# A hybrid encoder layer: TensorE's order in attention and recurrence is written by the program from a model of the other engines

## The chip, the cores and the metric

The kernel runs on one core of a Trainium2 chip. The metric is device time in microseconds (us) of one execution, the median of several; lower is better. The core has five engines that the profile names PE (TensorE: matrix products), DVE (VectorE), ACT (ScalarE), POOL (GpSimd) and SP (SyncE, which here only issues DMA transfers). Each works off its own queue in order and waits for the others by semaphores. SBUF is the on-chip memory of 128 partitions; a product lands in PSUM, of which one bank holds 128 x 512 float32 and must be copied out ("evicted") by another engine before it is used again.

## The reference, cut to what matters

One layer on 1024 frames of width 1024, all in float32.

```python
u = rms_norm(h, mix_norm_gain)
aq, ak, av, dqkv, dgate, da, db = split(u @ w_in)        # 8 attention heads of 64, 4 delta heads of 128
# A: every chunk of 64 frames looks at itself and the 8 chunks before it
q, k   = rms_norm(aq), rms_norm(ak)                      # per head
scores = q k^T * 64**-0.5 + rel_bias, masked to the band
o_att  = rms_norm(softmax(scores) @ v)
# B: gated delta rule, chunks of 64 in the reference; any chunk length gives the same result
dq, dk, dv = silu(causal_conv(dqkv));  q, k = l2_norm(dq) * 128**-0.5, l2_norm(dk)
T = I + strict(tril(beta k k^T * decay))                 # per chunk and head
value, k_cumdecay = T^-1 (beta v), T^-1 (beta k exp(decay))
for each chunk:                                          # S is the state, 128 x 128 per head
    v_new = value - k_cumdecay @ S
    o     = q_decay @ S + tril(q k^T * decay) @ v_new
    S     = S * chunk_decay + k_tail^T @ v_new
o_dn = rms_norm(o) * silu(dgate)
h = h + concat(o_att, o_dn) @ w_out
h = h + relu(rms_norm(h) @ w_ff1)**2 @ w_ff2
```

## The kernel before, in words

Frames are cut into 8 tiles or chunks of 128. The kernel goes through stages in the order of TensorE's time: the projection of dk (from 6 us), a small one for decay and beta, dq, dv, the gate, ak, aq, and six of the eight tiles of av; then attention and recurrence together (349 to 587 us), the output product `op` beside their end (562 to 662), and the two products of the feed-forward part (663 to 1281). Every large product is made of three (high x high, high x low, low x high part: `mm3`).

*Attention* goes over 16 tiles (g, t): g is a group of four heads, t one of 8 tiles of 128 frames. For each pair of heads pp (0 or 1), `score` makes the products with the keys, `t_sb` for the newest two tiles of keys and `t_sa` for up to three older ones, VectorE adds the bias and takes the row's extreme, and ScalarE the exponential (pages `t_pb`, `t_pa`). `value` transposes these on TensorE (`t_tpb`, `t_tpa`, into the two banks of `ps_t`), has them copied to SBUF (`t_tb` and the first `t_ta` by ScalarE, the second `t_ta` by VectorE), and multiplies by the values into one bank, `t_o`. The products into `t_o` use half of the array's columns each (128 x 64), so that two heads go side by side. `finish` turns `t_o` once more (`t_on`), and `turn` turns the normed result (`t_tpo`) for the output product.

*The recurrence* goes over 8 chunks c. Ahead of attention, beside the projections, `delta_prep` makes the matrices T and inverts their 32 x 32 diagonal blocks on VectorE (they go through memory: `x_dr`, `y_dr`, `a_dr`). In the stage, `delta_merge(c)` puts the blocks of one chunk together: first 32 x 32 products (`m_p`, four at a time on two corners of 32 x 32 of the array), then 64 x 64 ones (`m_tp`, `m_p`). `delta_state(c)` makes the products `c_tpv`, `c_pk`, `c_pv`, `c_pq` and `c_pS` with the state, `delta_out(c)` `c_tpq`, `c_mt`, `c_po`, and `delta_fin(c)` `c_tpo`. Each is a group of four products, one per head, in one of the two banks of `ps_d`.

What sets the order: these are Python generators, and `interleave` takes the next step from the one whose sum of given costs, divided by its weight, is least; the recurrence's own steps go in the order of a string of letters. This is the order in which the program names the instructions; a scheduler of the compiler then orders each engine's queue from it by its own model, and moves an instruction ahead of a neighbour where that model finds it ready earlier. So small groups of one kind come to stand between products of another:

```python
ORDER = "OSMOSMFSOMOSMSL"
...
    interleave((attention(after[NV - 1]), 1.0), (delta_all(ab, kT), 2.0), (values, WV))
    R, begun = out_proj()
```

At the start of the kernel, TensorE multiplies a page of ones `WARM` = 8 times (`warm`, line 111) while the first weights and the first part of x are loaded; `uh` and `wdk_h` are the high parts of x and of the first weights, made by ScalarE. ScalarE's first activation, line 185, brings a load of its function table with it.

Of the kernel before, what the change touches and what calls it, by code (L numbers as in the profile page):

```python
# [14 lines left out]
P = 128  # L15
# [7 lines left out]
ATT_D = 64  # L23
# [12 lines left out]
ORDER = "OSMOSMFSOMOSMSL"  # L36
LATE = 2
SPREAD = 5
WARM = 8
LAST = {"b22": "t1", "t3": "t2", "t4": "b22"}  # L40
RS = "a"
NV = 6
WV = 2.5
# [3 lines left out]
def hymba_kernel(  # L47
# [60 lines left out]
    nc.gpsimd.memset(ones, 1.0)  # L108
    warm = bank(ps_o, "warm")
# [51 lines left out]
    def mm3(ps, terms):  # L161
        n = 3 * len(terms)
        i = 0
        for (ah, al), (bh, bl) in terms:
            for a, b in ((ah, bh), (ah, bl), (al, bh)):
                nc.tensor.matmul(ps, a, b, start=(i == 0), stop=(i == n - 1))  # L166
                i += 1
# [8 lines left out]
    def load_xt(hf, k):  # L176
# [9 lines left out]
        nc.vector.scalar_tensor_tensor(lo, raw, mgain[:, k:k + 1], hi.bitcast(F32), ALU.mult, ALU.subtract)  # L186
        acc = squares[hf][k % 2]
# [7 lines left out]
    for k in range(NKT):  # L195
        if k:
            w_dk.append(load_w(w_in[k * P:(k + 1) * P, DK:DK + 512], f"wdk_{k}"))
        load_xt(0, k)
        if not k:
            w_dk.append(load_w(w_in[0:P, DK:DK + 512], "wdk_0"))  # L200
# [30 lines left out]
    nc.gpsimd.memset(state[0], 0.0)  # L231
# [259 lines left out]
    def delta_prep(kT, ab):  # L491
# [4 lines left out]
        for c in range(NT):  # L496
# [5 lines left out]
            kt = page("pp", n + "_kt")  # L502
            nc.vector.tensor_tensor(b4(kt), b4(tp), bc_row(ab["edec"][:, 1, h4]), ALU.mult)
            nc.sync.dma_start(out=kt_dr[c], in_=kt)
# [45 lines left out]
    def delta_merge(c, res):  # L550

        n = f"m{c}"
        Ap, Yp, s1 = (page("pp", n + k) for k in ("_ab", "_yb", "_s1"))
        A, Y = b4(Ap), b4(Yp)
        X = s1[:, 384:512].rearrange("p (h e) -> p h e", h=4)
        Yc = s1[:, 256:384].rearrange("p (h e) -> p h e", h=4)
        nc.sync.dma_start(out=Ap, in_=a_dr[c])
        for dst, src in ((X, x_dr), (Yc, y_dr)):
            nc.sync.dma_start(out=dst, in_=src[4 * c:4 * c + 4].rearrange("b r h e -> (b r) h e"))
        nc.gpsimd.memset(Yp, 0.0)  # L560
        for b in range(4):
            bs = slice(32 * b, 32 * b + 32)
            nc.gpsimd.tensor_copy(Y[bs, :, bs], Yc[bs])
        yield 0
        p1 = bank(ps_d, n + "_p1")
        for c0 in (0, 64):
            for h in range(4):
                nc.tensor.matmul(p1[c0:c0 + 32, 32 * h:32 * h + 32], A[c0:c0 + 64, h, c0:c0 + 32],
                                 Y[c0:c0 + 64, h, c0 + 32:c0 + 64], start=True, stop=True)
            nc.scalar.copy(s1[c0:c0 + 32, 0:128], p1[c0:c0 + 32, 0:128])  # L570
        yield 500
        p2 = bank(ps_d, n + "_p2")
        for c0 in (0, 64):
            cs = slice(c0, c0 + 32)
            for h in range(4):
                hs = slice(32 * h, 32 * h + 32)
                nc.tensor.matmul(p2[cs, hs], X[cs, h, :], s1[cs, hs], start=True, stop=True)
            nc.scalar.mul(Y[cs, :, c0 + 32:c0 + 64], p2[cs, 0:128].rearrange("p (h e) -> p h e", h=4), -1.0)
        yield 500
        tp = bank(ps_d, n + "_tp")  # L580
        for h in range(4):
            nc.tensor.transpose(tp[0:64, h * 64:h * 64 + 64], Y[0:64, h, 0:64], ident[0:64, 0:64])
        for h in range(4):
            nc.tensor.matmul(tp[0:64, 256 + h * 64:320 + h * 64], A[64:128, h, 0:64], Y[64:128, h, 64:128],
                             start=True, stop=True)
        x1 = s1
        nc.scalar.copy(x1[0:64, :], tp[0:64, :])
        yield 700
        p4 = bank(ps_d, n + "_p4")
        for h in range(4):  # L590
            hs = slice(h * 64, h * 64 + 64)
            nc.tensor.matmul(p4[0:64, hs], x1[0:64, hs], x1[0:64, 256 + h * 64:320 + h * 64],
                             start=True, stop=True)
        nc.scalar.mul(Y[0:64, :, 64:128], p4[0:64, 0:256].rearrange("p (h e) -> p h e", h=4), -1.0)
        res[c] = Yp
        yield 400

    def delta_state(c, ab, kTs, Ys, D):

# [8 lines left out]
        ktail = page("cv", n + "_kt")  # L608
        nc.sync.dma_start(out=ktail, in_=kt_dr[c])
# [3 lines left out]
        nc.vector.tensor_tensor(b4(rr), b4(tp), bc_row(ab["br"][:, h4]), ALU.mult)  # L613
        yield 500
        pk = bank(ps_d, n + "_pk")
        four(pk, lambda h, hs: kT[:, hs], lambda h, hs: S[:, h, :])
        for h in range(4):
            hs = slice(h * P, (h + 1) * P)
            nc.vector.scalar_tensor_tensor(
                rr[:, hs], pk[:, hs], ab["nbr"][:, 4 * c + h:4 * c + h + 1], rr[:, hs],  # L620
                ALU.mult, ALU.add)
        yield 900
# [4 lines left out]
        nc.scalar.copy(vn, pvn)  # L627
        yield 900
        pq = bank(ps_d, n + "_pq")
        four(pq, lambda h, hs: dq[:, hs], lambda h, hs: S[:, h, :])  # L630
        o = page("cv", n + "_o")
        nc.vector.tensor_tensor(b4(o), b4(pq), bc_row(ab["edec"][:, 0, h4]), ALU.mult)
        yield 900
        pS = bank(ps_d, n + "_pS")
        four(pS, lambda h, hs: ktail[:, hs], lambda h, hs: vn[:, hs])
        for h in range(4):
            nc.vector.scalar_tensor_tensor(
                S2[:, h, :], S[:, h, :], ab["edec"][:, 2, 4 * c + h:4 * c + h + 1],
                pS[:, h * P:(h + 1) * P], ALU.mult, ALU.add)
        D[c] = dq, dg, vn, o  # L640
        yield 900

    def delta_out(c, ab, kTs, D):
# [4 lines left out]
        dq, dg, vn, o = D.pop(c)  # L648
        Lt = decay(T, n + "_Lt", ab, h4, tri_u, tri_sr, nc.gpsimd)
        nc.gpsimd.tensor_tensor(b4(Lt), b4(Lt), bc_mask(tri_u), ALU.mult)  # L650
        yield 450
        tp = bank(ps_d, n + "_tpq")
        four_t(tp, head(dq))
        nq = rsqrt("c", sumsq(tp, "c", tp, n + "q"), 4, 1.0, EPS, n + "q")
# [4 lines left out]
        yield 500  # L659
# [3 lines left out]
        nc.vector.tensor_tensor(att, mp, Lt, ALU.mult)  # L663
        yield 900
        po = bank(ps_d, n + "_po")
        four(po, lambda h, hs: att[:, hs], lambda h, hs: vn[:, hs])
        nc.vector.tensor_tensor(o, o, po, ALU.add)
        ss = sumsq(po, "c", o, n)
# [5 lines left out]
        yield 900  # L674

    def delta_fin(c, D):
        n = f"c{c}"
        o, dg = D.pop(c)
        tp = bank(ps_d, n + "_tpo")
        four_t(tp, head(o))  # L680
        if c % TPH == 0:
            mix[c // TPH][1] = quarter(f"mixd{c // TPH}")
        nc.vector.scalar_tensor_tensor(q4(mix[c // TPH][1])[:, :, (c % TPH) * P:(c % TPH + 1) * P], b4(tp), dng,
                                       b4(dg), ALU.mult, ALU.mult)
        yield 500

    def delta_all(ab, kTs):

        Ys, D = {}, {}
        merge = delta_merge(0, Ys)  # L690
        yield from merge
        merge = delta_merge(1, Ys)
        for c in range(NT + LATE):
            gens = dict(S=delta_state(c, ab, kTs, Ys, D) if c < NT else iter(()),
                        O=delta_out(c - 1, ab, kTs, D) if 0 < c <= NT else iter(()),
                        F=delta_fin(c - LATE, D) if c >= LATE else iter(()), M=merge)
            merge = delta_merge(c + 2, Ys) if c + 2 < NT else iter(())
            gens["L"] = merge
            for k in ORDER:
                cost = next(gens[k], None)  # L700
# [707 lines left out]
```

## Time and profile before

| | |
|---|---|
| time, median of 3 runs | 1286.75 us (1284.92 to 1287.67) |
| the profiled execution | 1288.31 us, its span 1286.6 us |
| mean granted clock of TensorE | 0.998 of full speed |
| busy share of the span | PE 98%, DVE 73%, ACT 43%, POOL 23% |
| DMA | 160.65 MB in 129288 packets, 125 GB/s over the span |

The profile's page gives the busy time of each engine, the span in slices, the chain of work that ended last, and groups of instructions by line. A row of the timeline gives the start in us from the span's start, the time that a run of equal instructions took, engine, line, operation, tiles (written <- read), the part of the array in use (rows*columns), the shape, the number of records, and in brackets the idle time ahead of it with what ended that. A float32 product on TensorE often shows as two records.

### The profile page before, as it was taken

The page shows a single profiled execution, that of the slowest core. Times are in us where ns is not written, and L with a number is a line of the kernel's source. Part 1 is how long each engine was busy: PE and PEld are TensorE (multiplying, and loading weights), DVE is VectorE, ACT ScalarE, POOL GpSimd, SP SyncE. Part 2 cuts the span into 40 slices and gives each one's busy share as a digit, 9 for nine tenths or more (in the row PEclk, how much of TensorE's full clock was granted, in tenths as well). Part 3 has the DMA queues.
Part 4 walks back from the last instruction along what each step waited for, and adds up shares of the span by engine and source line. Part 5 has one row for each costly group of instructions (what it writes and reads, how often), then busy time and mean ns, then how long its engine had stood idle before and what let it go on. Part 6 is the DMA issues. An engine that isn't in the chain of part 4 may idle for free.

```text
span 1286.6 us, 18043 instructions
## 1 busy us (share of the span) xinstructions
PE 1260.6 (98%) x6702; PEld 1040.6 (81%) x6702; DVE 935.0 (73%) x1401; ACT 553.9 (43%) x919; POOL 293.0 (23%) x499
## 2 busy tenths in 40 slices
PE   9999999999999999989999999999999999999998
PEld 7778878788888887868877788888887888888886
DVE  7899987665046666863529876776668997897988
ACT  7233132133166664665335445444455443333331
POOL 4435461454024355523310000000000000000034
PEclk9999999999999999999999999999999999999999
DMA  6214353656492742125351433232358733422002
GB/s 223 61 44 140 100 164 112 145 147 160 144 270 79 218 109 75 42 65 163 122 166 31 151 116 129 98 110 97 105 196 318 238 93 104 131 86 95 17 33 98
DMA packets 129288, 160.65 MB, mean 125 GB/s; under 512 B 22832, under 2 KB 71984, under 8 KB 128688
## 3 DMA queue, kind: packets, MB, share of 16 engines
q1 hardware_dynamic: 111104, 137.20, 34.7%
q10 hardware_dynamic: 18096, 22.29, 5.0%
q8 instruction: 53, 0.87, 0.3%
q14 instruction: 35, 0.29, 0.1%
HBM read 111.75 MB, written 47.71 MB: 124 GB/s over the span
## 4 chain that ended last, share of the span: by engine, by line
PE 72%; DVE 8%; issue 2%; DMA 2%; POOL 1%; ACT 1%; POOLq 1%; SPq 0%; ACTq 0%; DVEq 0%
PE q L1087 22%; PE p L1183 20%; PE op L166 5%; PE av_ps L166 3%; PE aq_ps L166 3%; PE g_ps L166 3%; PE t_o L865 3%; PE ak_ps L166 2%; PE t_sb L793 1%; PE t_sa L793 1%; PE t_tpb L844 1%; PE t_tpa L855 1%; PE c_mt L461 1%; PE c_pS L461 1%; DVE ml L148 1%
## 5 line engine op out<-in xcount | busy, mean ns | idle before, releaser
L1255 POOL TENSOR_TENSOR y<-y,y 128x1024 f32<-128x1024 f32 x6 | 19.3, 3243 | 591.7 <-DVE y L1251 572.9
L1251 DVE TENSOR_TENSOR y<-y,p 128x1024 f32<-128x1024 f32 x46 | 55.2, 1218 | 5.4 <-PE p L1183 4.5
L808 DVE CUSTOM_DVE_ANT_0 t_pb<-t_sb,biasn 128x256 f32<-128x256 f32 (+1 forms) x64 | 25.4, 402 | 43.6 <-POOL biasn L720 25.4
L166 PE MATMUL op<-mh,wo_h 128*128 128x512 f32 x128 | 50.3, 393 | 0.8 <-DVE t_nm L808 0.3
L166 PE MATMUL op<-ml,wo_h 128*128 128x512 f32 x128 | 50.1, 391 | 0.0
L166 PE MATMUL op<-mh,wo_l 128*128 128x512 f32 x128 | 48.3, 391 | 0.0
L823 ACT ACTIVATE t_pb<-t_pb,t_nm 128x256 f32<-128x256 f32 (+1 forms) x64 | 31.6, 494 | 22.7 <-DVE t_nm L817 12.7
L966 DVE TENSOR_TENSOR h<-op,op_x 128x512 f32<-128x512 f32 x16 | 10.8, 688 | 30.7 <-PE op L166 30.7
L793 PE MATMUL t_sb<-ks,t_q 128*128 128x256 f32 (+1 forms) x144 | 30.4, 308 | 0.8 <-DMA t_q<-q_dr 0.5
L973 POOL TENSOR_TENSOR op_q<-op_q 128x512 f32<-128x512 f32 x14 | 20.1, 1439 | 48.0 <-ACT op_q L972 47.8
L166 PEld LDWEIGHTS op<-mh,wo_h 128*128 128x128 f32 x128 | 24.0, 188 | 7.4 <-issue 1.0
L817 DVE CUSTOM_DVE_ANT_0 t_pa<-t_sa,biaso,t_nm 128x384 f32<-128x384 f32 (+2 forms) x48 | 26.3, 547 | 4.4 <-PE t_sa L793 2.9
L865 PE MATMUL t_o<-t_ta,vt 128*64 128x128 f32 x240 | 27.3, 293 | 1.4 <-DVE t_ta L858 1.1
L166 PEld LDWEIGHTS op<-mh,wo_l 128*128 128x128 f32 x128 | 24.0, 188 | 5.2 <-issue 0.2
L166 PEld LDWEIGHTS op<-ml,wo_h 128*128 128x128 f32 x128 | 24.0, 188 | 4.9
L166 PE MATMUL g_ps<-uh,wg_h 128*128 128x512 f32 x64 | 25.2, 394 | 1.4 <-ACT wg_h L147 1.4
L826 ACT ACTIVATE t_pa<-t_pa,t_nm 128x384 f32<-128x384 f32 (+2 forms) x48 | 26.4, 550 | 0.1
L793 PE MATMUL t_sa<-ks,t_q 128*128 128x256 f32 (+2 forms) x128 | 25.5, 310 | 0.3 <-DVE t_nm L808 0.3
L166 PE MATMUL g_ps<-uh,wg_l 128*128 128x512 f32 x64 | 25.2, 394 | 0.4 <-POOL wg_l L148 0.4
L166 PE MATMUL dq_ps<-uh,wdq_h 128*128 128x512 f32 x64 | 25.5, 398 | 0.0
L166 PE MATMUL dv_ps<-uh,wdv_l 128*128 128x512 f32 x64 | 25.4, 397 | 0.0
L166 PE MATMUL aq_ps<-waq_h,uh 128*128 128x512 f32 x64 | 25.3, 401 | 0.0
(1102 smaller groups left out, 4353.8 us busy)
## 6 DMA issues: line engine op xcount, KB each, us to landing
wa<-in_w_ff_dram SPq DMA_DIRECT2D x32, 512.0 KB
a<-in_w_ff_dram SPq DMA_DIRECT2D x32, 512.0 KB
b<-f_dr SPq DMA_DIRECT2D x32, 512.0 KB
f_dr<-yy ACTq DMA_DIRECT2D x16, 512.0 KB
t_q<-q_dr SPq DMA_DIRECT2D x30, 256.0 KB
f_dr<-zz ACTq DMA_DIRECT2D x13, 512.0 KB
ks<-k_dr SPq DMA_DIRECT2D x16, 256.0 KB
wo_r<-in_w_out_dram SPq DMA_DIRECT2D x16, 256.0 KB
```

Of the source, the lines that this page charges most:

```text
L166: nc.tensor.matmul(ps, a, b, start=(i == 0), stop=(i == n - 1))
L461: nc.tensor.matmul(ps[:, hs], lhs(h, hs), rhs(h, hs), start=True, stop=True)
L793: nc.tensor.matmul(o, q[m][:, i * P:(i + 1) * P], k[:, c], start=(m == 0), stop=(m == 1))
L808: nc.vector.tensor_tensor_reduce(sb[:, c], bk[:, c], new[g][pp][:, c], -1.0, 3.0e38, ALU.add, ALU.min, nm[:, 4 + i:5 + i])
L817: nc.vector.tensor_tensor_reduce(sa[e][:, 0:wa], bk[:, 0:wa], old[g][i][:, 384 - wa:384], -1.0, nm[:, 4 + i:5 + i], ALU.add, ALU.min, nm[: ...
L823: nc.scalar.activation(sb[:, c], sb[:, c], AF.Exp, bias=m, scale=-1.0, accum_out=T["sums"][:, 4 + i:5 + i])
L826: nc.scalar.activation(sa[e][:, 0:wa], sa[e][:, 0:wa], AF.Exp, bias=m, scale=-1.0, accum_out=T["sums"][:, i:i + 1])
L865: nc.tensor.matmul(po[64 * e:64 * e + 64, pp * P:(pp + 1) * P], vt[k0 + j][:, 64 * h:64 * h + 64], (ta[e] if j < na else tb)[:, c:c + P], ...
L973: nc.gpsimd.tensor_tensor(acc, acc, sq, ALU.add)
L1087: nc.tensor.matmul(part(ps, q), l[:, s], r, start=(k + m == 0), stop=(k == 3 and m == 2))
L1183: nc.tensor.matmul(part(ps[q], 0) if by_rows else part(ps[q // 2], q % 2), l[:, s], part(r, k), start=(i + k + m == 0), stop=(i + k + m == 4))
L1251: nc.vector.tensor_tensor(y[i][m], y[i][m], ps[m], op)
```

## The change

*The order.* A class `Clock` holds a model: the time on TensorE (`pe`), the intervals in which VectorE, ScalarE and POOL are taken (`on`), and the time from which each PSUM bank is free again (`give`). `attention` no longer yields to `interleave`. It has a loop of its own that keeps a list of what may come next: steps of the recurrence, `multiply` (the products into `t_o` for both pairs of heads of a tile), `later` (`finish` and `turn`), `flip` (the transposes), `score`, the rest of `av`, and, once the values are all turned, steps of the output product, which is now a generator. It takes the one that the model says can start first, by rank where several can. The loop runs under `manual_schedule` for TensorE, so the order of the program is TensorE's order; the other engines' queues are still ordered by the scheduler.

*The evictions* are named under `high_priority`, and the copies of `t_tb` and `t_ta` go to the one of VectorE and ScalarE that the model says is done sooner (`sooner`).

*The merges.* `delta_low` does the 32 x 32 steps for four chunks at once (`l_p`, 32 products behind each other); for the first four chunks it stands ahead of the stage, beside the projections. `delta_merge` keeps the 64 x 64 steps. The blocks are loaded from memory in more and smaller transfers.

*Less work.* In chunk 0, where the state is zero, `c_pk` and `c_pq` go, and the state is copied, not added to. In chunk 7 `c_pS` and its operand `kt` go.

*The start.* `WARM` is 11; an activation of one column of ones (`turn_on`) stands ahead of all others on ScalarE; the load of the first weights `wdk_0` is named earlier. In the norm ahead of the feed-forward part, a reciprocal gets priority.

The diff, cut to its core:

```diff
-ORDER = "OSMOSMFSOMOSMSL"
-WARM = 8
+WARM = 11
+DELTA = 71e3
+LATENCY, MARGIN = 250, 400
-WV = 2.5
+class Clock:
+    def pe(self, cost):
+        self.now += cost
+        return self.now + LATENCY
...
+    def sooner(self, costs, *after):
+        def end(e):
+            t = max((self.now,) + after)
+            for a, b in self.free[e]:
+                if a <= t < b:
+                    t = b
+            return t + costs[e]
+        return min(costs, key=end)
+
+    def give(self, pool, t):
+        self.banks[pool].pop(0)
+        self.banks[pool].append(t)
+        return t + MARGIN
...
+    turn_on = cpool.tile([P, 1], F32, name="turn_on")
+    nc.scalar.activation(turn_on, ones[:, 0:1], AF.Square)
...
+    def delta_low(b, W, tag):
...
+        for c in range(4):
+            q = 16 * b + 4 * c
+            for k in range(4):
+                nc.sync.dma_start(out=Y[c // 2][32 * k:32 * k + 32, c % 2, :, 32 * (k % 2):32 * (k % 2) + 32],
+                                  in_=y_dr[q + k])
+            for r0 in (0, 64):
+                nc.sync.dma_start(out=XA[r0:r0 + 32, c], in_=x_dr[q + r0 // 32])
+                nc.sync.dma_start(out=XA[r0 + 32:r0 + 64, c], in_=a4[c, r0 + 32:r0 + 64, :, r0:r0 + 32])
...
+            held(places, lambda c, h, hs: nc.tensor.matmul(
+                p1[rs, hs], XA[rs2, c, h, :], Y[c // 2][rs2, c % 2, h, 32:64], start=True, stop=True))
+            with tc.high_priority():
+                nc.scalar.copy(s1[rs], p1[rs])
...
-        pk = bank(ps_d, n + "_pk")
-        four(pk, lambda h, hs: kT[:, hs], lambda h, hs: S[:, h, :])
+        if c:
+            yield max(t, when["state"]), "d"
+            pk = bank(ps_d, n + "_pk")
+            four(pk, lambda h, hs: kT[:, hs], lambda h, hs: S[:, h, :])
...
-            nc.scalar.copy(*w3)
+            t = pe(nb * 218)
+            e = clock.sooner(dict(s=140 + nb * 220, v=160 + nb * 270), t)
+            with tc.high_priority():
+                copy[e](*w3)
+            t = give("t", on(e, 140 + nb * 220, t, ahead=True))
...
+        while True:
...
+            best = min(todo, key=lambda p: (max(p[0] - clock.now, 0), p[1]))
+            if best[0] > clock.now:
+                clock.now = best[0]
...
+            elif k == "multiply":
+                for n in units[multiplied:multiplied + 2]:
+                    multiply(*n)
+                    pe(218 * size[multiplied])
...
-                with tc.issue_after(m.ins):
+                with tc.issue_after(m.ins), tc.high_priority():
                     nc.vector.reciprocal(r_col, r_col)
...
-        (delta_prep(kT, ab), 0.35))
-    interleave((attention(after[NV - 1]), 1.0), (delta_all(ab, kT), 2.0), (values, WV))
-    R, begun = out_proj()
+        (chained(delta_prep(kT, ab), (1000 for _ in delta_low(0, W, "pp"))), 0.35))
+    clock.reset()
+    with tc.manual_schedule(engines={mybir.EngineType.PE}):
+        rest = attention(after[NV - 1], delta_all(ab, kT, W), values, lambda: out_proj(result))
+    for _ in rest or ():
+        pass
```

How this moves TensorE's instructions shows best at one tile's products into `t_o`. This is TensorE's queue at the tile (g, t) = (0, 5) in the order before; the names are the transposed pages `t_ta` and `t_tb` of two heads and the value tiles `vt`:

```order
L461 MATMUL c_po<-c_vn,c_att 128x128 x4
L865 MATMUL t_o<-t_ta_5134,vt_3469 64x128
L844 MATMUL t_tpb_5343<-ident,t_pb_5076 128x128 x4
L865 MATMUL t_o<-t_ta_5140,vt_3469 64x128
L865 MATMUL t_o<-t_ta_5134,vt_3799 64x128
L865 MATMUL t_o<-t_ta_5140,vt_3799 64x128
L865 MATMUL t_o<-t_ta_5134,vt_3802 64x128
L865 MATMUL t_o<-t_ta_5140,vt_3802 64x128
L865 MATMUL t_o<-t_tb_5128,vt_3813 64x128 x2
L865 MATMUL t_o<-t_tb_5128,vt_3816 64x128
L461 MATMUL c_pq<-state_297,c_jq 128x128 x4
L865 MATMUL t_o<-t_tb_5128,vt_3816 64x128
```

And the same tile now:

```order
L672 MATMUL m_tp<-ident,l_w_4324 64x64 x4
L674 MATMUL m_tp<-l_w_4324,m_sa 64x64 x4
L1009 MATMUL t_o<-t_ta_4674,vt_3582 64x128
L1009 MATMUL t_o<-t_ta_4680,vt_3582 64x128
L1009 MATMUL t_o<-t_ta_4674,vt_3755 64x128
L1009 MATMUL t_o<-t_ta_4680,vt_3755 64x128
L1009 MATMUL t_o<-t_ta_4674,vt_3758 64x128
L1009 MATMUL t_o<-t_ta_4680,vt_3758 64x128
L1009 MATMUL t_o<-t_tb_4616,vt_3769 64x128 x2
L1009 MATMUL t_o<-t_tb_4616,vt_3772 64x128 x2
L1009 MATMUL t_o<-t_ta_4719,vt_3582 64x128
L1009 MATMUL t_o<-t_ta_4747,vt_3582 64x128
```

The transposes `t_tpb` and the group `c_pq`, which stood inside the products of one pair of heads, are gone from there, and the second pair's products follow at once.

The merges, on TensorE again, where the second 32 x 32 products of chunk 5 stood before, at the beginning of the second group of heads:

```order
L865 MATMUL t_o<-t_tb_5737,vt_3466 64x128 x2
L461 MATMUL c_pk<-state_297,kT_654 128x128 x4
L865 MATMUL t_o<-t_tb_5762,vt_3466 64x128 x2
L577 MATMUL m_p_4622<-m_s_4547 32x32 x4
L887 MATMUL t_on<-ident,t_pb_5724 128x128 x2
L844 MATMUL t_tpb_5797<-ident,t_pb_5750 128x128 x4
L577 MATMUL m_p_4622<-m_s_4547 32x32 x4
L465 MATMUL c_tpo<-ident,c_o 128x128 x4
```

And where the second batch of them, for chunks 4 to 7, has its second product now:

```order
L515 MATMUL c_pv<-c_jv,m_yb 128x128 x4
L515 MATMUL c_pq<-state_302,c_jq 128x128 x4
L1031 MATMUL t_on<-ident,t_pb_4155 128x128 x2
L970 MATMUL t_tpb_4611<-ident,t_pb_4233 128x128 x4
L648 MATMUL l_p_4618<-l_s_4327,l_xa 32x32 x32
L515 MATMUL c_pS<-c_vn,c_kt 128x128 x4
```

Fours of 32 x 32 products between others on the whole array have become one run of 32.

The beginning of ScalarE's queue, before:

```order
L1403 UNCONDITIONAL_BRANCH
L180 DMA xt_174<-in_x_t_dram 128x512
L185 ACT_TABLE_LOAD
L185 ACTIVATE uh_0_150<-xt_174,mgain 128x512
L190 ACTIVATE xs_179<-xt_174 128x512
```

And now:

```order
L1649 UNCONDITIONAL_BRANCH
L235 DMA xt_179<-in_x_t_dram 128x512
L163 ACT_TABLE_LOAD
L163 ACTIVATE turn_on<-ones 128x1
L240 ACTIVATE uh_0_155<-xt_179,mgain 128x512
```

The table load no longer stands with the first activation that needs x, but with one that needs only the ones.

More of the change, by code (lines that the diff above doesn't have):

```diff
@@ L165, in mm3 @@
             for a, b in ((ah, bh), (ah, bl), (al, bh)):
-                nc.tensor.matmul(ps, a, b, start=(i == 0), stop=(i == n - 1))
+                nc.tensor.matmul(ps, a, b, start=(first and i == 0), stop=(last and i == n - 1))
                 i += 1
@@ L607, in delta_state @@
             nc.sync.dma_start(out=b4(t), in_=src[c])
[L608 to L609 removed]
+        if c + 1 < NT:
+            ktail = page("cv", n + "_kt")
+            nc.sync.dma_start(out=ktail, in_=kt_dr[c])
+        yield clock.now + 2000, "d"
         tp = bank(ps_d, n + "_tpv")
@@ L910, in attention, with live_add @@
-        for i in range(len(units) + lag + late):
-            if i < len(units):
-                g, t, pp = units[i]
+        size = [min(t + 1, 5) for g, t, pp in units]
+        total, spent, deltas, begun, multiplied = sum(size), 0, 0, 0, 0
+        ready, later, live = [], [], {}
+        banks = clock.banks
+        groups = delta
+        fed = next(groups)
+        def live_add(name, gen):
+            first = next(gen, None)
+            if first is not None:
+                live[name] = gen, first
```

425 lines of the change are left out of this document (296 added, 129 removed).

## The prediction

> **What bounds the kernel now.** I read the page's busy shares first, then the busy time in stretches of the attention and recurrence stage, then TensorE's instructions there in order of time.
>
> ```profile
> PE 1260.6 (98%) x6702; PEld 1040.6 (81%) x6702; DVE 935.0 (73%) x1401; ACT 553.9 (43%) x919; POOL 293.0 (23%) x499
> PE 72%; DVE 8%; issue 2%; DMA 2%; POOL 1%; ACT 1%; POOLq 1%; SPq 0%; ACTq 0%; DVEq 0%
> ...
> 349.00:400.00 51.00, 51.00 (x440) 42.78 (x441) 22.78 (x92) 28.71 (x91) 14.89 (x46) 1.00 0.75 220
> 400.00:450.00 50.00, 50.00 (x501) 43.77 (x497) 31.48 (x100) 32.12 (x93) 20.12 (x58) 1.00 0.50 154
> 450.00:500.00 50.00, 47.60 (x449) 39.93 (x448) 32.61 (x103) 29.45 (x92) 25.98 (x71) 1.00 0.39 104
> 500.00:562.00 62.00, 58.69 (x532) 50.64 (x530) 48.70 (x134) 40.00 (x109) 28.20 (x77) 0.97 0.13 36
> 562.00:590.00 28.00, 25.04 (x149) 19.63 (x148) 14.67 (x26) 11.64 (x26) 9.82 (x17) 1.00 0.44 132
> ```
>
> TensorE is busy for 98% of the span and is 72% of the chain. In the stage's stretches (columns: stretch, length, then busy PE, PEld, DVE, ACT, POOL, the granted clock, DMA) it is idle for only 0 + 0 + 2.40 + 3.31 + 2.96 = 8.7 us; VectorE is busy at most 48.70 of 62 us. So an order that only removed idle time could win 8.7 us. But a busy TensorE is not one at its peak, so I looked at how far apart the starts lie:
>
> ```profile
> 420.90 1.16 PE L461 MATMUL c_po<-c_vn,c_att 128*128 128x128 f32 x8
> 421.99 0.43 PE L865 MATMUL t_o<-t_ta,vt 128*64 128x128 f32 x2
> 422.35 0.66 PE L844 MATMUL t_tpb<-ident,t_pb 128*128 128x128 f32 x4
> 422.94 0.76 PE L865 MATMUL t_o<-t_ta,vt 128*64 128x128 f32 x9
> ...
> 423.96 1.16 PE L461 MATMUL c_pq<-state,c_jq 128*128 128x128 f32 x8
> 425.05 0.43 PE L865 MATMUL t_o<-t_tb,vt 128*64 128x128 f32 x2
> ...
> 433.61 0.38 PE L887 MATMUL t_on<-ident,t_pb 128*128 128x128 f32 x2
> 433.83 0.60 PE L844 MATMUL t_tpb<-ident,t_pb 128*128 128x128 f32 x4
> 434.26 0.49 PE L465 MATMUL c_tpq<-ident,c_jq 128*128 128x128 f32 x3
> ```
>
> The first column is the start, 128*64 the part of the array in use. Four transposes between others on the whole array take 434.26 - 433.83 = 0.43 us. The same four between two t_o groups take 422.94 - 422.35 = 0.59 us, though no idle time is shown. They pay 0.16 us for coming from and going to another array form. I did this for every matmul of the stage: the start-to-start distance, less what its kind has inside a run of one form.
>
> ```profile
> 349.28 0.33 PE L793 MATMUL t_sb<-ks,t_q 128*128 128x128 f32 x2
> ...
> 425.75 0.49 PE L855 MATMUL t_tpa<-ident,t_pa 128*128 128x128 f32 x3
> 426.00 0.49 PE L793 MATMUL t_sb<-ks,t_q 128*128 128x256 f32 x2
> ...
> 587.05 0.60 PE L465 MATMUL t_tpo<-ident,t_on 128*128 128x128 f32 x4
> ```
>
> From the first t_sb (349.28) to the last t_tpo (587.05) the form changes 174 times, and the excess there adds to 25.6 us, 0.147 us each. That is three times the idle time, and no wait shows it.
>
> **The change, part by part.**
>
> *Fewer changes of form.* I counted runs of one form in the order: 175 before and 61 now in this stretch, so 114 changes fewer. t_o now comes in 16 blocks (it had 51 runs), and the 25 runs of 32x32 products are two. At 0.147 us that is 16.8 us, all on TensorE's own path, with nothing to hide it. Bounds: 0.10 us each (what t_o loses on leaving) makes 11; 0.20 (c_pq takes 425.05 - 423.96 = 1.09 us; its records stand 0.111 us apart inside the run, and eight times that is 0.89) makes 23. I keep the mean. [...] Ahead of the stage five runs less give 5 x 0.147 = 0.7 us.
>
> *Work removed.* Chunk 0 has no state, so its c_pk and c_pq go, and so does chunk 7's c_pS: three groups of four products. A group is eight records in the trace, 0.111 us apart as above: 0.9 us, and 2.7 us for three. VectorE loses twelve 128-column operations and three 512-column ones and gains two copies, POOL issues 16 operations less, ScalarE 20; all three have idle time in every stretch above, so I cost these at nothing.
>
> *Idle time and evictions.* Evictions go ahead in their queues, and TensorE keeps the order written down even where something is not ready.
>
> ```profile
> 550.96 0.66 PE L844 MATMUL t_tpb<-ident,t_pb 128*128 128x128 f32 x4 [0.87 <-DVE mixa L904]
> ...
> 553.20 0.80 PE L855 MATMUL t_tpa<-ident,t_pa 128*128 128x128 f32 x3 [0.79 <-ACT t_tb L847]
> ...
> 565.56 0.66 PE L844 MATMUL t_tpb<-ident,t_pb 128*128 128x128 f32 x4 [0.90 <-ACT t_on L893]
> ...
> 569.53 0.76 PE L865 MATMUL t_o<-t_ta,vt 128*64 128x128 f32 x9 [1.15 <-DVE t_ta L858]
> 549.90:553.40 3.50, 1.84 (x15) 1.45 (x14) 1.78 (x6) 2.65 (x8) 1.50 (x6) 0.99 0.00 0
> 553.40:556.80 3.40, 3.40 (x21) 2.41 (x21) 2.88 (x8) 1.78 (x5) 0.00 (x0) 0.50 0.00 0
> 563.60:567.00 3.40, 2.16 (x16) 1.58 (x15) 1.37 (x4) 2.27 (x8) 1.12 (x4) 1.00 0.84 286
> ```
>
> The largest waits lie at the end, when the recurrence is over and attention alone waits for its copies. In the new order chunk 7's products stand among the last tiles, and steps of the output product follow. Idle time can fall by all 8.7 us, or grow as much where an order that can't bend meets a late copy. I take a third off: -3. After 1.66 us idle between 549.9 and 553.4 the clock fell to 0.50 for 3.4 us, which cost 1.7 us; with that cluster spread out I take -1.7 (bounds: 0, or one more such fall, +1.7).
>
> *The merges' loads.* The lower 32x32 merges of four chunks become one step; the first moves ahead of attention. SP issues 46 DMAs more in all (480 to 526 in the order). Around the start of the q projection 24 small loads stand where 7 larger ones stood, ahead of its last weights:
>
> ```profile
> 251.82 1.10 SPq L559 DMA_DIRECT2D m_s<-y_dr  x2
> 253.49 6.95 SPq L447 DMA_DIRECT2D k_dr<-ak_l  x4
> 262.77 3.09 SPq L154 DMA_DIRECT2D waq_r<-in_w_in_dram  x3
> ```
>
> At up to 0.5 us each, 17 more take 8.5 us of SP. SP has some 2.3 us free there now (the k_dr stores end at 253.49 + 6.95 = 260.44, the weights begin at 262.77), and part of the 6.95, in which two pairs of stores of the row are issued with a wait between them. If all of it showed, TensorE would wait 8.5 us for the weights, or as long for the loads themselves, since the products stand in a fixed place; hidden, it is 0. I take +1, as the queue has most of that room.
>
> *The start.*
>
> ```profile
> 1.05 3.78 PE L111 MATMUL warm<-ones 128*128 128x128 f32 x16 [1.05 <-POOL ones L108]
> 6.30 0.79 PE L307 MATMUL dk_ps<-uh,wdk_h 128*128 128x512 f32 x1 [1.47 <-ACT wdk_h L147]
> 6.89 0.63 PE L307 MATMUL dk_ps<-ul,wdk_h 128*128 128x512 f32 x1
> 7.32 0.63 PE L307 MATMUL dk_ps<-uh,wdk_h 128*128 128x512 f32 x1
> ...
> 9.88 1.46 PE L307 MATMUL dk_ps<-uh,wdk_l 128*128 128x512 f32 x4
> 11.17 1.07 PE L307 MATMUL dk_ps<-uh,wdk_h 128*128 128x512 f32 x4
> ...
> 3.20 1.28 ACT L185 ACT_TABLE_LOAD   x1 [3.20 <-DMA mgain<-in_mix_norm_gain_dram]
> ```
>
> The table load (1.28 us) moves into ScalarE's wait for x, so uh and wdk_h come 1.28 us earlier, at about 5.0. Each warm product is two records; the first is 0.37 us ahead of the second and the rest stand 0.2135 us apart (from start to start in the trace). The last of 22 would be followed at 1.05 + 0.37 + 21 x 0.2135 = 5.9, so the first real one starts 0.4 us earlier, with no gap before it. Its distance is 0.43 us at half clock; in the row at 9.88 they fall to 0.23, from 10.6 on: this is the end of the first 3.41 us stretch without a gap (553.4 lies 159 such stretches later). Without the gap that end is one stretch earlier, at 7.2. The twelve products then take until 9.3 instead of 11.2: -1.8 (bounds: -0.4 if the clock rises no sooner, -2.3). [...]
>
> *No cost or gain.* The reciprocal's priority in norm_col: the order leaves it behind the same four operations, so the row
>
> ```profile
> PE hrow L1051 <- DVE r_col L1045: 1.7, 1, 1.7
> ```
>
> stays. From ff1 on the order is nearly the same (a few VectorE operations swap), so the part behind its first product,
>
> ```profile
> 662.95 0.47 PE L1087 MATMUL q<-b11h,q_0a_h 128*128 128x512 f32 x1 [0.88 <-DVE h L966]
> ```
>
> stays within 1 us.
>
> **Sum:** -1.8 - 0.7 + 1 - 16.8 - 2.7 - 3 - 1.7 = -25.7 us, or 2.0%. The profiled execution took 1288.31 us, 1.7 more than its span of 1286.6; it would take 1262.6. The median of three runs is 1286.75, 1.56 under the profiled one; on it the sum gives 1261.
>
> **Rivals.**
>
> *New waits eat much of it.* Each of the 16 t_o blocks now needs up to six copies done at once, and one PSUM bank serves them. One wait of 1 us at each, as at 569.53, costs 16 us and makes 1277; a wait of 0.6 makes 1271. For it: that wait, and VectorE's 79% in 500 to 562. Against: two transpose groups and the scores stand between copy and use. 0.17.
>
> *The price is no price of form.* If the excess came from loading weights after a jump, it would come back elsewhere: 1261 + 16.8 = 1278. Against: the t_tpa that t_sb follows on the whole array, at 425.75, take 426.00 - 425.75 = 0.25 us for three, no excess. 0.07.
>
> *The waits all go,* 8.7 instead of 3, and the SP loads hide: 1254 or less. 0.09.
>
> *Slower:* one mechanism, the fixed order at the t_o blocks. Sixteen waits of 1.6 us cancel the gain; from 1.8 us on the kernel is slower, 1.9 us makes 1291. The longest wait of the stage now is 1.15 us. 0.04.
>
> *No change to speak of,* between those two: 0.03.
>
> *The clock falls in transposes.* The new order has a run of 23 transposes, about 2.5 us. [...] Were such runs to halve it, each fall would cost 1.7 us; three make 1266. Between 563.6 and 567.0 TensorE did little but some fifteen transposes and 1.24 us of idling, and the clock stayed 1.00; the trace speaks against it. 0.02, inside the likeliest case's range.
>
> **The numbers.** The sum as it stands, give or take 7 us for waits and loads (1254 to 1268 or so), has 0.60. Reaching to half of the first two rivals and most of the third gives 1251 to 1277 for 8 in 10. About 0.2%, 2.6 us, is what a measurement can tell from no change: faster 0.60 + 0.17 + 0.07 + 0.09 = 0.93, same 0.03, slower 0.04.
>
> **What would show it.** Right: the first dk product near 5.9 and distances of 0.23 from about 7.2; t_o in 16 blocks; four transposes 0.43 apart nearly everywhere; the first ff1 product near 637 instead of 663, and 624 us from there to the end as before. Wrong: waits at t_o or t_tpa of a microsecond each, a gap at the first aq product or the first l_p, or stretches at clock 0.50 in the stage.

## The result, and the profile after

The changed kernel is slower: 1319.55 us median of five runs (1308.9 to 1323.4) against 1286.75 (1284.92 to 1287.94), a ratio of 1.0239 (95% interval 1.0214 to 1.0265). The forecast was 1261. The profiled execution is the quickest of the five, 1308.9 us with a span of 1307.1. Its page and the stretches of the stage, in the columns shown for the kernel before:

```profile
PE 1249.8 (96%) x6684; PEld 1038.5 (79%) x6684; DVE 933.2 (71%) x1389; ACT 548.1 (42%) x899; POOL 289.9 (22%) x486
PE 57%; DVE 8%; ACT 2%; issue 2%; POOL 2%; DMA 1%; POOLq 1%; SPq 0%; DVEq 0%; ACTq 0%
...
349.00:400.00 51.00, 43.95 (x331) 36.90 (x330) 21.04 (x87) 26.55 (x87) 12.77 (x41) 0.97 0.71 209
400.00:450.00 50.00, 43.70 (x482) 39.15 (x480) 26.19 (x80) 25.54 (x72) 16.63 (x47) 0.96 0.44 126
450.00:500.00 50.00, 42.40 (x400) 37.21 (x400) 31.47 (x99) 26.43 (x81) 21.43 (x54) 1.00 0.30 81
500.00:550.00 50.00, 39.19 (x341) 35.98 (x341) 31.22 (x97) 24.76 (x77) 16.18 (x48) 0.93 0.23 64
550.00:610.00 60.00, 50.94 (x388) 43.02 (x389) 37.00 (x79) 29.36 (x70) 30.98 (x68) 0.97 0.20 62
```

TensorE is idle for 7.0 + 6.3 + 7.6 + 10.8 + 9.1 = 40.8 us of these stretches; from 349 to 610 us of the kernel before it is 9.0. No other engine is busier than before. The clock is below 1.00 in four stretches of five. The summed waits of TensorE in the stage (total, times, longest) name the place, and the last row is what the first one was before:

```profile
PE t_sb L914 <- DVE t_nm L930: 23.2, 31, 1.5
PE t_tpa L986 <- ACT t_ta L991: 3.5, 1, 3.5
PE t_tpa L986 <- ACT t_tb L976: 2.4, 4, 1.0
...
PE t_sb L793 <- DVE t_nm L808: 0.2, 1, 0.2
```

And one of the 31, in the timeline:

```profile
402.19 0.48 PE L914 MATMUL t_sb<-ks,t_q 128*128 128x256 f32 x2
...
402.71 0.42 DVE L930 CUSTOM_DVE_ANT_0 t_pb<-t_sb,biasn 128x256 f32<-128x256 f32 x1
403.06 0.08 DVE L930 DVE_READ_ACCUMULATOR2_ANT t_nm<- 128x1 f32 x1
...
403.19 0.50 PE L914 MATMUL t_sb<-ks,t_q 128*128 128x256 f32 x2 [0.53 <-DVE t_nm L930]
403.54 0.86 PE L914 MATMUL t_sa<-ks,t_q 128*128 128x384 f32 x4
```

`score` puts the newest keys' products of two heads into the two halves of one bank. The program names them as product, VectorE's reduction, product, reduction, and the second product waits until VectorE has read the first half. In the trace of the changed kernel nothing stands between the two heads' products in any of the 32 banks. Before, the scheduler put other products into that gap. One bank of the kernel before, with its first product, VectorE's read of it, and its second product 7.4 us behind the first:

```profile
417.99 0.48 PE L793 MATMUL t_sb<-ks,t_q 128*128 128x256 f32 x2
...
420.54 0.41 DVE L808 CUSTOM_DVE_ANT_0 t_pb<-t_sb,biasn 128x256 f32<-128x256 f32 x1
...
425.41 0.51 PE L793 MATMUL t_sb<-ks,t_q 128*128 128x256 f32 x2
...
425.95 0.42 DVE L808 CUSTOM_DVE_ANT_0 t_pb<-t_sb,biasn 128x256 f32<-128x256 f32 x1
```

The trace does not name the banks; that these two share one follows from the program, where `score` takes one bank for each pair of heads, and from the order of the reads. The next t_sb, at 426.00 in the prediction's rows, is the first of another pair: it starts 0.05 us behind the start of the read of 425.95, with no idle time shown. So the wait is seen where the bank is shared: 0.53 us at 403.19 in the changed kernel, 23.2 us in all 31. The prediction should have asked for it; the kernel before has it once, for 0.2 us, in the last row of the waits above.

A wait costs more than the idle time shown. From 402.39, the start of the first product's second record, to 403.19 are 0.80 us: 0.53 idle, 0.12 what such a record takes in a run, and 0.16 more. For 31 waits that is 5 us on top of the 23.2. This document calls it a restart.

### The profile page after: what moved, and what is told of

Its sections match the earlier page's. It is cut to its first block, busy times and chain, and to the rows that moved or that the text cites. A ratio compares the mean times of both kernels' runs of the same rounds, so it can differ in the third digit from the quotient of the medians.

```text
span 1307.1 us, 18026 instructions
## 1 busy us (share of the span) xinstructions
PE 1249.8 (96%) x6684; PEld 1038.5 (79%) x6684; DVE 933.2 (71%) x1389; ACT 548.1 (42%) x899; POOL 289.9 (22%) x486
## 4 chain that ended last, share of the span: by engine, by line
PE 57%; DVE 8%; ACT 2%; issue 2%; POOL 2%; DMA 1%; POOLq 1%; SPq 0%; DVEq 0%; ACTq 0%
PE q L1329 21%; PE p L1425 20%; PE op L221 5%; PE t_o L1009 2%; PE t_sb L914 1%; PE t_sa L914 1%; PE t_tpb L970 1%; PE c_pv L515 1%; DVE t_pb L930 1%; PE t_tpa L986 1%; PE c_pq L515 1%; POOLq L1649 1%; PE c_pS L515 0%; POOL wo_l L203 0%; DVE y L1497 0%
## 5 line engine op out<-in xcount | busy, mean ns | idle before, releaser
L914 PE MATMUL t_sb<-ks,t_q 128*128 128x256 f32 (+1 forms) x144 | 32.6, 320 | 23.8 <-DVE t_nm L930 23.2
L914 PEld LDWEIGHTS t_sb<-ks,t_q 128*128 128x128 f32 x144 | 21.5, 195 | 30.3 <-DVE t_nm L930 29.9
L986 PE MATMUL t_tpa<-ident,t_pa 128*128 128x128 f32 x120 | 21.9, 295 | 8.4 <-ACT t_ta L991 3.5
```

The lines of the kernel that those rows point to most:

```text
L914: nc.tensor.matmul(o, q[m][:, i * P:(i + 1) * P], k[:, c], start=(m == 0), stop=(m == 1))
L986: nc.tensor.transpose(tp[:, js], sa[e][:, js], ident)
```

## The experiments

All times are medians in us against the kernel before in the same session (1286.6 to 1287.8).

| label | kernel | median | ratio (95%) |
|---|---|---|---|
| e1_both_first | changed, both heads' products ahead of the reductions | 1296.66 | 1.0077 (1.0062 to 1.0092) |
| e3_scheduler | changed, TensorE's queue left to the scheduler | 1280.48 | 0.9952 (0.9936 to 0.9969) |
| e5_spread | before, 48 extra products one by one | 1314.58 | 1.0213 (1.0196 to 1.0230) |
| e5_block | before, the same 48 in eight runs | 1298.93 | 1.0110 (1.0078 to 1.0141) |
| e4_start | before, the start's edits alone | 1288.01 | 1.0000 (0.9991 to 1.0009) |
| e7_both | e1 and e3 together | 1278.15 | 0.9927 (0.9913 to 0.9941) |
| e8_margin | e1, margin 1500 | 1289.99 | 1.0019 (1.0007 to 1.0030) |
| e9_no_priority | e1, no priorities | 1297.37 | 1.0075 (1.0061 to 1.0088) |
| e10_margin_q | e8, the t_q loads of two tiles from ScalarE's queue | 1289.75 | 1.0016 (1.0005 to 1.0027) |
| e11_both_q | e7, the same loads from there | 1277.56 | 0.9927 (0.9910 to 0.9945) |
| e12_both_q_margin | e11, margin 1500 | 1275.81 | 0.9915 (0.9895 to 0.9935) |
| e13_loads | e8, the model told of t_q's load | 1284.35 | 0.9978 (0.9969 to 0.9988) |

### The wait in the shared bank

```diff
...
                 cost += product(g, T, i, bk, c.start, kb, t + 1)
+                landed.append(pe(30 + wb * 0.9))
+            for e in range(2):
...
                 nc.vector.tensor_tensor_reduce(sb[:, c], bk[:, c], new[g][pp][:, c], -1.0, 3.0e38, ...)
-                done.append(on("v", 180 + wb * 1.25, pe(30 + wb * 0.9)))
+                done.append(on("v", 180 + wb * 1.25, landed[1]))
```

The edit moves the reductions and, in the model, the time at which they are done, so the order behind it is not quite the same either.

> The changed kernel with one edit: in score, both heads' products into the t_sb bank are named before VectorE's two reductions of that bank, so that the second head's product no longer stands behind VectorE's read of the first. Theory A (the wait of the second t_sb product for VectorE in the same bank, 23.2 us of TensorE's idle time in 31 waits, is most of what went wrong, and the clock's falls, mean 0.993 in the profiled run and 0.980 to 0.985 in the others, follow from it): t_sb's waits for t_nm fall from 23.2 to below 4 us, TensorE's idle time in the stage from 40.8 to about 20 us, and the time from 1319.6 to 1283 to 1297. Rival B (the order as a whole runs ahead of the copies, so the idle time only moves to t_tpa, t_tpb or t_o): t_sb's waits go, the idle time stays above 33 us and the time above 1312.

1296.66, 22.9 us less than the changed kernel, at the upper end of what theory A gave; rival B's time is out. The waits of t_sb for t_nm are gone. But the idle time in the stage fell only to 29.8 us, not 20, so a part of it did move, as B says. The clock is no higher (0.985 to 0.988 in its four runs, 0.980 to 0.993 in the five of the changed kernel), so its falls did not come from these waits alone, against what theory A says. The waits, in the same view:

```profile
PE t_sb L914 <- DMA t_q<-q_dr: 7.4, 1, 7.4
PE t_tpa L991 <- ACT t_tb L981: 6.1, 5, 3.1
PE t_tpa L991 <- DVE t_ta L996: 3.5, 1, 3.5
```

A new wait of 7.4 us has come for one load of t_q, as the scores reach tile (0,2) sooner than its load does. The clock is at one half from 369.4 to 386.4 us, which costs 8.5 us (the first stretches of it):

```profile
366.20:369.60 3.40, 0.71 (x3) 0.28 (x2) 1.42 (x9) 2.37 (x11) 0.00 (x0) 0.97 1.05 390
369.60:373.00 3.40, 0.00 (x0) 0.00 (x0) 0.00 (x0) 0.00 (x0) 0.00 (x0) 0.50 1.07 299
373.00:376.40 3.40, 2.00 (x10) 1.92 (x12) 0.77 (x5) 0.00 (x0) 0.00 (x0) 0.50 1.06 220
376.40:379.80 3.40, 3.40 (x24) 2.78 (x25) 0.64 (x6) 2.69 (x10) 0.00 (x0) 0.50 0.15 55
```

### The order left to the scheduler

```diff
-    with tc.manual_schedule(engines={mybir.EngineType.PE}):
+    if True:
         rest = attention(...)
```

> The changed kernel without the manual schedule: the steps are named in the same order, but the compiler's scheduler may reorder TensorE's queue again (158 runs of one array form in the stage instead of 61, 175 in the kernel before). Theory A (the fixed order makes the waits; the rest of the change costs nothing): waits at t_sb below 3 us, idle time in the stage near the 8.7 us of before, form changes cost 97 x 0.147 = 14 us again: 1274 to 1288. Rival C (the new merges, the evictions' priority or the loads cost by themselves): above 1295.

1280.48, inside theory A's range and 39 us below the changed kernel. The largest waits of the stage:

```profile
PE l_p L639 <- DMA l_xa<-a_dr: 2.2, 1, 2.2
...
PE t_tpa L986 <- ACT t_on L1038: 0.8, 1, 0.8
```

From 349 to 610 us there are 7.2 us of idle time and none at t_sb. So less work, the new merges, their loads, the copies' new places and the start cost nothing as a whole; together they win 0.5%. What lost was the fixed order. The ten runs reach from 1277.07 to 1286.18, and the profiled one is the slowest: behind the wait for `l_xa` and the first merges (407.5 to 421.2 us) its clock is at one half, which costs 6.8 us.

Both edits together:

> Both edits together: both heads' products ahead of the reductions, and the scheduler free to reorder TensorE. Theory A (with the scheduler the wait was filled already, in the kernel with that edit alone it is 0): no more than the form changes saved, 157 to 142 runs or 2 us: 1277 to 1281. Rival E (the edit has a worth of its own, since the softmax of a pair of heads starts earlier): below 1275.

1278.15, as theory A had it; the edit that won 22.9 us under the fixed order wins 2.3 here, where the two intervals just overlap. The wait is worth so much only where nothing may move into it.

### The price of a change of form

```diff
+        def extra(n):
+            for _ in range(n):
+                nc.tensor.matmul(spare[0:64, 0:P], ones[:, 0:64], ones, start=True, stop=True)
...
                 for k in range(NKT):
...
+                    if k < 6:
+                        extra(1)
```

These lines, behind the three products of each k, are those of e5_spread; e5_block has `if k == 5: extra(6)` there. Theory A is that each change of form costs 0.147 us, the mean of the stage before: 96 changes against 16 then make 80 x 0.147 = 11.8 us between the two kernels. Rival D is that the excess comes from something else than form, such as weights loaded after a jump: below 2 us.

> The kernel before with 48 small extra products of ones (128 x 64 of the array, into a bank that nobody reads) in the gate projection, where TensorE has no idle time; here one alone after every three products, so 96 changes of array form. [...]

> The kernel before with the same 48 extra products in eight runs of six. By the spacing of t_o's records (0.055 us a record, two to four records a product) 48 products take 5 to 11 us, and 16 changes of form 2.4 us: 1294 to 1300. Theory A: 11.8 us less than with the 48 one by one; rival D: within 2 us of it.

The difference is 15.65 us, more than the 11.8 of theory A. Some of the time is clock: summed over the profiled execution, (1 - granted clock) x time is 7.2 us with the 48 apart and 1.9 in eight runs, and the falls lie far behind the gate projection (at 477, 593 and 1013 us). The rows of the gate projection have none of that (first the 48 apart, then in runs):

```profile
170.48 0.43 PE L352 MATMUL spare<-ones 128*64 128x128 f32 x2
170.85 0.50 PE L361 MATMUL g_ps<-uh,wg_h 128*128 128x512 f32 x1
171.18 0.39 PE L361 MATMUL g_ps<-ul,wg_h 128*128 128x512 f32 x1
171.41 0.40 PE L361 MATMUL g_ps<-uh,wg_l 128*128 128x512 f32 x1
171.74 0.43 PE L352 MATMUL spare<-ones 128*64 128x128 f32 x2
```

```profile
171.69 1.52 PE L352 MATMUL spare<-ones 128*64 128x128 f32 x12
173.14 0.50 PE L361 MATMUL g_ps<-uh,wg_h 128*128 128x512 f32 x1
173.48 0.39 PE L361 MATMUL g_ps<-ul,wg_h 128*128 128x512 f32 x1
173.71 0.40 PE L361 MATMUL g_ps<-uh,wg_l 128*128 128x512 f32 x1
173.94 0.39 PE L361 MATMUL g_ps<-uh,wg_h 128*128 128x512 f32 x1
```

One product between two triples takes 171.74 - 170.48 - 3 x 0.23 = 0.57 us; inside a run it takes two records at 0.109, or 0.22. Two changes thus cost 0.35, 0.17 us each. Over the projection, from its first product to its last, 75.7 against 62.2 us make 13.5 for 80 changes, again 0.17. Rival D is out.

### The start

```diff
-WARM = 8
+WARM = 11
+    turn_on = cpool.tile([P, 1], F32, name="turn_on")
+    nc.scalar.activation(turn_on, ones[:, 0:1], AF.Square)
```

(and the load of `wdk_0` named ahead, as in the change)

> The kernel before with the three edits of the start alone (11 warm products, the activation that brings the table load early, the load of the first weights named earlier). The prediction's term says 1.8 us less (bounds 0.4 and 2.3): 1284.9. The trace of the changed kernel has its 13th product of dk at 8.22 us instead of 11.17, so a gain of 2.9 us that nothing later gives back: 1283.8. If a later stage gives it back (the projections wait for weights anyway): 1286 to 1287.

1288.01 against 1287.83: nothing. Its trace has the 13th product of dk at 8.06 us, where it was 11.17, and the 49th at 18.35 instead of 19.34: two waits for weights, 0.5 and 1.0 us, have come, and 2.1 of the 3.1 us are back by then. At the first t_sb the kernel is 1.8 us ahead (347.46 against 349.28), at the first ff1 product 1.3 (661.7 against 663.0), and in this execution ff2 gives them back in a stretch at half clock (988 us, 1.7 us).

### The copies

```diff
-LATENCY, MARGIN = 250, 400
+LATENCY, MARGIN = 250, 1500
```

> The kernel with both heads' products first, and in the model that writes the order a margin of 1500 ns instead of 400 between the end of a copy and the step that needs it. Of its 29.8 us idle in the stage 7.4 are for t_q's load and some 15 for copies of t_tb, t_ta, t_on and the mixed pages. Theory F (the model takes the copies for sooner than they are by a microsecond or so): these 15 fall to below 8, the time from 1296.7 to 1282 to 1291. Rival G (single copies are late by 3 us and more, as they stand behind others in their queue, where the model has no idea of them): the time stays within 4 us of 1296.7.

1289.99: 6.7 us less than e1, inside theory F's range. The waits for t_tb, t_ta, t_on and the mixed pages fell from 13.6 to 10.1 us, not below 8: the two longest, 3.1 and 3.5 us, are gone (the longest is now 1.5), and others have come in their place. More came from the clock (12.3 us lost to it against 20.7), so F's time is right and its reason holds in part. The same kernel as e1 without priorities:

> The kernel with both heads' products first, without any of the priorities of evictions (TensorE's order is the same). Theory H (the priority keeps copies from standing behind other work): waits of TensorE for ScalarE's and VectorE's copies rise by 8 us or more: above 1304. Rival I (the scheduler puts them there anyway, since its model has TensorE waiting for them): within 4 us of 1296.7.

1297.37 against e1's 1296.66: rival I. Here the priority of evictions does nothing that can be measured. Why a copy can be late all the same shows in e1's ScalarE and TensorE rows:

```profile
556.53 1.64 ACT L202 CAST wo_h<-wo_r 128x512 fp32r<-128x512 f32 x3
558.08 0.57 ACT L981 COPY t_tb<-t_tpb 128x512 f32<-128x512 f32 x1
558.55 0.47 ACT L996 COPY t_ta<-t_tpa 128x384 f32<-128x384 f32 x1
558.71 0.55 PE L991 MATMUL t_tpa<-ident,t_pa 128*128 128x128 f32 x3 [3.14 <-ACT t_tb L981]
```

The copy stands behind three casts of output weights, which the model that wrote TensorE's order does not know; the queue of ScalarE is the scheduler's. So what G says of single copies is seen here, though in e8 the larger margin left no such long wait for them.

### The load of t_q

```diff
-                    nc.sync.dma_start(out=qf[r0:r0 + 64]..., in_=q_dr[t, :, :, g, :])
+                    (nc.scalar if not g and 1 < t < 4 else nc.sync).dma_start(out=qf[r0:r0 + 64]..., in_=q_dr[t, :, :, g, :])
```

> The fixed order with both heads' products first and the margin of 1500 ns, and the loads of t_q for tiles (0,2) and (0,3) issued from ScalarE's queue instead of SP's, where they stood behind 4 loads of ks, 3 of vt and a store that waits for av_s. Theory J (the 7.1 us wait for t_q at 376 is SP's queue, and the fall of the clock behind it, 5.1 us of the 12.3 that the clock takes in this kernel, comes from that wait): the wait falls below 2 us, the fall goes with it, and 1290.0 becomes 1276 to 1281. Rival K (the 16 DMA engines are full there, so the load lands late from any queue): the wait stays above 5 us, the time within 3 us of 1290.

1289.75, no change: rival K's time. The first of the loads is issued 3.4 us sooner than in e8 (366.07 against 369.47), and the product that needs them starts 3.3 us sooner (373.04 against 376.37). So it is 7 us from issue to use from either queue, and the queue is not what makes these loads take long. The wait is still 5.0 us, and 2.1 us have come at a transpose that needs an exponential which ScalarE begins behind the load's issue, at 366.68. Under the scheduler:

> The kernel with the scheduler and both heads' products first, with the same two loads from ScalarE's queue. It waits 3.0 us for a t_q load at 396, with a fall of the clock of 1.7 us behind it; but that is a later tile than the two moved. Theory J: 1274 to 1278; rival K: within 2 us of 1278.2.

1277.56, within 2 us of e7. The wait for t_q is gone here, but 1.4 us at transposes have come and the clock takes 8.9 us of the profiled execution instead of 5.9: K's time, not its reason.

> The same with the margin of 1500 ns in the model. Where the scheduler reorders TensorE anyway the margin should matter little: form runs go from 142 to 154 (12 x 0.147 = 1.8 us more), waits for t_tb and t_ta (2.2 us) fall by a microsecond: within 3 us of the kernel without it.

1275.81, within 3 us of e11, as expected; their intervals overlap. Its profiled execution, the quickest of four, has a span of 1269.9 us, 5.1 us idle in the stage and a clock of 0.999. Its median is the lowest here, 0.85% below the kernel before.

```diff
...
+                q_at = scored[-2] + (7000 if begun < 8 else 4000) if pp == 0 and len(scored) > 1 else 0
-                todo.append((max(a[0], a[1] - 500, a[2] - 900, START if not begun else 0), 4, "score"))
+                todo.append((max(a[0], a[1] - 500, a[2] - 900, q_at, START if not begun else 0), 4, "score"))
...
+                if pp:
+                    scored.append(clock.now)
```

> The fixed order with both heads' products first and the margin of 1500 ns, and a model that knows of t_q's load: the scores of a tile may start only 7 us (for the first four tiles, 4 us later on) behind the scores of the tile whose page they reuse. Theory L (the order asks for t_q too early because the model has no loads in it, and other steps could stand there): the 7.1 us wait for t_q and the clock's fall of 5.1 us behind it shrink by half or more, 1290.0 becomes 1278 to 1285. Rival M (at that place TensorE has nothing else that is ready: two pages of t_q bound it, and the wait only moves to another operand): within 3 us of 1290.

1284.35, 5.6 us less than e8 and at the end of theory L's range: the wait for t_q falls only from 7.1 to 4.7 us, the fall of the clock behind it from 5.1 to 3.4. L and M both hold in part. This is the only fixed order that beats the kernel before, by 0.22% (0.12% to 0.31%).

## Why the prediction was wrong

Against the profiled execution the sum gave 1262.6, and 1308.9 was measured: 46.3 us more. By the same working on both traces, each from end to end:

- *Changes of form:* forecast 16.8 us in the stage and 0.7 ahead of it. The excess at changes is 27.8 us before and 9.1 after: 18.7. This term was right, in mechanism and size, and e5 shows a price of this size, 0.17 us, by itself.
- *Idle time:* this is the step that failed, the -3. The prediction took a third off 8.7 us and put the danger at the t_o blocks. TensorE's idle time over the whole span rose from 20.7 to 52.1 us, 34 more than forecast with the 3 us; at t_o it is below 0.1. The pairs of t_sb make 23.2 us of it; the largest of the others is one wait of 3.5 us for a t_ta. The sum took the waits of the old order as a measure for the new one. It never asked which products had become neighbours, though the order has all 32 pairs of t_sb side by side with VectorE's read between them. e1 shows that the pairs are the cause of 23 us, and e3 that only the fixed order makes them cost.
- *Restarts:* not in the sum. What the products ahead of a wait take beyond their time in a run adds to 5.4 us before and 10.4 now, 5 us more.
- *The clock:* forecast -1.7. (1 - granted clock) x time went from 4.1 to 10.5 us in the profiled execution, with four falls in the stage instead of one. They begin at 397.33, 431.46, 527.04 and 564.58, and two of them, each with the stretch ahead of it, are:

```profile
428.58 1.19 PE L648 MATMUL l_p<-l_s,l_xa 32*32 32x32 f32 x32
430.50 1.27 PE L648 MATMUL l_p<-l_s,l_xa 32*32 32x32 f32 x32 [0.73 <-ACT l_w L652]
428.05:431.46 3.41, 2.68 (x68) 2.40 (x67) 0.86 (x2) 1.39 (x4) 2.13 (x4) 1.00 0.43 149
431.46:434.88 3.42, 3.42 (x23) 3.36 (x20) 1.06 (x4) 1.07 (x3) 0.74 (x2) 0.50 0.02 5
523.63:527.04 3.41, 0.63 (x5) 0.58 (x5) 1.92 (x9) 3.34 (x11) 0.00 (x0) 1.00 0.00 0
527.04:533.86 6.82, 5.60 (x25) 5.34 (x24) 3.99 (x12) 4.00 (x13) 4.74 (x15) 0.50 0.26 73
```

  That is 8 us beside the forecast. The later fall follows 2.78 us of idle time, the wait of 3.5 us for a t_ta. The earlier one follows only 0.73 us: most of the rest of its stretch is the batch of 32 x 32 merges that the change made. In e1 a fall at 270.39, ahead of the stage, follows 0.57 us of idle time and 54 such records. So the batched merges seem to have a price in clock that the prediction did not ask for; no run takes them out, so how much is not shown. The clock also accounts for the median, which lies 10.7 us above the profiled execution: the five runs have mean clocks of 0.993, 0.984, 0.980, 0.985 and 0.983 and times of 1308.9, 1319.55, 1323.4, 1319.12 and 1320.17, and 0.009 of 1318 us are 11.9.
- *Start and loads:* the start's -1.8 was more at the 13th product (8.22 against 11.17) and is worth 1 us or nothing at the end (e4). The clock rose at 4.80 us, not at 7.2; in the eleven traces with this start it rises between 4.2 and 6.9. No wait came at the first l_p or at aq, so the +1 for the loads was not needed there.
- *Work removed:* what is left of the span without changes of form, idle time, restarts and falls of the clock is 3.6 us shorter than before, and some 5 us in e3; the forecast for work, start and loads was -2.7 - 1.8 + 1 = -3.5.

34 + 8 + 5 - 1 (form) makes 46. Of the rivals, "new waits" and "slower" had the right kind of mechanism, waits that a fixed order can't fill, but at the t_o blocks and for late copies instead of a bank that is still being read, and with too little chance (0.17 and 0.04). That transposes halve the clock is not seen: in e3 a stretch of 3.40 us (561.10 to 564.50) with 13 transposes, nothing else and 1.45 us of idle time kept it at 1.00.

Open is what a fixed order could reach. e13 has 60 runs of one form, the changed kernel 61, and still 21.5 us idle in the stage; e12 has 154 runs and 5.1. No run had both few changes and few waits, so the forecast 1261 was not reached by any.

## What to carry to other kernels

When an order is frozen, list the pairs that become neighbours on the frozen engine and look for another engine's work between them in the program, above all a read of the same PSUM bank; a scheduler that may move things hides such a pair (0.2 us of waiting in the kernel before), a fixed order pays for it every time (23.2 us in the changed kernel). A model that fixes one engine's order needs the real queues of the others and the loads; in this kernel its order did better as a proposal to the scheduler (e7, e12). Count a wait as its idle time, a restart (0.16 us here), and the clock that may fall behind it (1.7 us for each stretch of 3.41 us at one half here).

## What the runs showed of the hardware

- A change between products on the whole array and products on 128 x 64 of it costs 0.17 us (e5: 13.5 us for 80 changes), with no idle time shown; the mean over all forms in the stage before is 0.147.
- The clock falls to 0.50 at the end of a stretch of 3.41 us, and stays there for one (553.36 to 556.78 in the kernel before) to five such stretches (369.4 to 386.4 in e1). In the traces of this case every stretch behind the first 10 us with more than 2.1 us of idle time was followed by one at 0.50 (2.78 us ahead of 527.04 in the changed kernel). With 1.3 to 1.9 us some were (1.66 us ahead of 553.36 in the kernel before, 1.80 ahead of 564.58 in the changed kernel, 1.78 in ff2 of e3, ahead of 984.4) and some were not (1.65 us ahead of 700.14 in the kernel before, 1.76 ahead of 1008.32 in the changed kernel). Falls behind less were seen where small products took much of the rest: 0.73 us beside 62 records of 32 x 32 in the changed kernel (ahead of 431.46), 0.57 beside 54 in e1 (ahead of 270.39), 0.90 beside twelve of 64 x 64 in the changed kernel (ahead of 397.33). A stretch with 0.72 us and 39 such records of 32 x 32 (ahead of 424.64 in the changed kernel) kept the clock.
- Runs of one kernel differ with the clock, and idle time alone does not tell by how much: 1.1% in the changed kernel (mean clocks 0.980 to 0.993), 0.7% in e3, 0.2% in e13 with its 21.5 us idle, 0.2 to 0.4% in the kernel before.
- A wait of TensorE costs about 0.16 us more than its idle time (mean over the 32 pairs of t_sb in the changed kernel).
